# Layer two's probabilities turned by way of DRAM, its value products three panels behind, and three panels at once at the head of a stage

## The chip, the cores and the metric

The kernel runs on one core of a Trainium2 chip. The metric is device microseconds of one execution, the median of some runs. Engines are called as in the profile: PE is TensorE (PEld its weight loads), DVE VectorE, ACT ScalarE, POOL GpSimd; SP only issues DMAs. Every engine works through its own queue in order and waits at an instruction until what it needs is there.

## The reference, cut to what matters

Two decoder layers over 256 tokens of width 2048, all in float32. Layer 1 mixes with gated linear attention (GLA), layer 2 with forgetting attention (FoX, 12 heads of 128, keys and values computed once before the layer). Each layer also attends with four heads to 256 memory tokens, and each ends with a gated MLP of 5632 hidden units with a causal convolution of width 3.

```python
def memory_attention(q, mem_k, mem_v):            # 4 heads, 256 x 256 probabilities
    s = einsum('bhqd,bhkd->bhqk', heads(q), mem_k) * HD ** -0.5
    return merge(einsum('bhqk,bhkd->bhqd', softmax(s), mem_v))

def fox_attention(q, k, v, c):                    # 12 heads, causal
    s = einsum('bhqd,bhkd->bhqk', q, k) * HD ** -0.5
    s = s + c[t] - c[s]                           # sums of log forget gates
    return einsum('bhqk,bhkd->bhqd', softmax(where(causal, s, -inf)), v)

def fox_mixer(h, fk, fv, fc, mem_k, mem_v, w_in, w_out):
    q, mq = split_cols(h @ w_in, [1536, 512])
    return concat([fox_attention(q, fk, fv, fc),
                   memory_attention(mq, mem_k, mem_v)]) @ w_out

for i in range(2):                                # i = 0: gla_mixer, i = 1: fox_mixer
    x = x + mixer(rmsnorm(x), ...)
    u = causal_dwconv(rmsnorm(x) @ w_up[i])       # a, val = halves of u
    x = x + (silu(a) * val) @ w_down[i]
return rmsnorm(x)
```

## The kernel before, in words

**Weights and panels.** Every projection is cut into panels, a panel into units of 128 x 1024 float32 (512 KB). `split_unit` (lines 189 to 208) loads a unit into one of four `raw` buffers by a DMA from SP, rounds it on ACT to an fp32r part `whi` and subtracts that on DVE to give `wlo`; there are four buffers of each. So the kernel can hold four split units and four raw ones ahead of PE. Activations lie feature-major as two fp32r parts side by side (`bufA`, `bufB`: 16 tiles of 128 x 2 x 256, one for each block of 128 features). `proj_fm` computes 256 output features of all 256 tokens (4 units): per unit 8 matmuls of 512 columns with `whi` (line 242) and 8 of 256 columns with `wlo` (line 240). `proj_tm` (line 285) computes token-major panels of up to 512 features (8 units of 12 matmuls).

**Order.** The program is traced once; a planner gives each engine its fixed order by simulated time and by a priority that is the place in the program. `tc.high_priority(offset)` moves a piece forward by `offset` places (`AHEAD` is 300; unit loads and casts carry it), `tc.issue_after` ties an instruction behind another on its engine.

**The head of a stage.** The stages before the two MLPs and before FoX end with a token-major product added to `x` (`add_out`, four panels f = 0 to 3). After each, `preparing.then(f, b)` adds the squares for the norm, turns 32 x 32 blocks of `x` on DVE (line 1006, `blk`), moves the blocks between partitions with 16 DMAs (`move`, line 434, tile `turn`) and splits the result into the next stage's input (`split_turned`: ACT line 331, DVE line 333). For f = 3 all this has priority 2 x AHEAD, half of the moves are issued from ACT, and the norm's row (`n.row`, PE line 400, ACT line 403) is made with priority. The next stage starts with `pair_fm`: of two panels the units 0 to 2 come first, which need only feature blocks 0 to 11, and unit 3 of both (blocks 12 to 15, which come from f = 3) last. The second panel accumulates in the two PSUM banks of tag "s".

**Layer 2's attention.** `fox` takes eight query panels of two heads: two of memory queries, then six of FoX queries. When a panel ends, its evacuation makes q and scores (PE lines 455 for memory, 908 and 909 for FoX), the softmax on DVE and ACT, and turns the probabilities on PE against an identity matrix (`turn_blocks`, line 477: four 128 x 128 blocks for a memory head, three for a FoX head, PSUM bank "t"). A copy brings them to SBUF (ACT line 922; for memory the two parts of lines 441 and 442), the product with the values follows on PE (lines 455, or 925 and 926, bank "o"), and `split` writes the head's two parts into `mix`. The output projection (`("wo", 1, f)`) reads `mix` blocks 12 to 15 first, then 0 to 11.

**GLA.** For a head, `core` computes the scores inside the head, `outputs` the product with values and `scale` the norm; the order of the heads' pieces on PE is tied by `issue_after`.

Of the kernel before, what the change touches and what calls it, by code (L numbers as in the profile page):

```python
# [12 lines left out]
F32 = mybir.dt.float32  # L13
F32R = mybir.dt.float32r
# [5 lines left out]
P = 128  # L20
# [120 lines left out]
def _trunk(ctx: ExitStack, tc: tile.TileContext, xt, xtok, memt, wp, wgu, gns, gfin, cnv, par, msk, out):  # L141
# [71 lines left out]

    def pair_fm(keys, src, evacs):

        head = [(u, low) for u, low in ((0, 0), (1, 0), (0, 1), (1, 1), (2, 1), (2, 0))]
        panels_fm(keys, src, evacs, [(p, *t) for p in range(2) for t in head]
                  + [(0, 3, 0), (0, 3, 1), (1, 3, 1), (1, 3, 0)])

    def panels_fm(keys, src, evacs, turns, between=None):  # L220

        units = [where[key] for key in keys]

        acc = [[work("s", 2) if p else pacc.tile([P, 512], F32, name="acc", tag="acc") for _ in range(2)]
               for p in range(len(keys))]
        base = min(min(u[1]) for u in units[0])
        ready = {}
        for at, (p, u, low) in enumerate(turns):
            if (p, u) not in ready:
                ready[p, u] = split_unit(units[p][u])  # L230
                if u == 1 and between is not None:
                    between()
            end = all(t[0] != p for t in turns[at + 1 :])
            w = ready[p, u][low]
            for j, kc in enumerate(units[p][u][1]):
                both = src[kc - base]
                for c in range(2):
                    s = slice(j * 256 + c * P, j * 256 + (c + 1) * P)
                    if low:
                        TE.matmul(acc[p][c][:, :T], w[:, s], both[:, 0, :], start=False, stop=end and j == 3)  # L240
                    else:
                        TE.matmul(acc[p][c], w[:, s], both, start=u == j == 0, stop=end and j == 3)  # L242
# [13 lines left out]
    def proj_tm(key, src, evac, spare=None, first=None):  # L256
# [10 lines left out]
        for i in range(len(units) + ahead):  # L267
# [13 lines left out]
            for b, u, low, j in steps:  # L281
                kcs = units[u][1]
                w = ready[u][low][:, j * n : (j + 1) * n]
                for part in range(2 - low):
                    mm = TE.matmul(acc[b][:, :n], src[kcs[j] - base][:, part, b * P : (b + 1) * P], w,  # L285
                                   start=u == 0 and low == part == j == 0,
                                   stop=u == end and low == 1 and j == len(kcs) - 1)
                if u == end and low and j == len(kcs) - 1:
                    ends.append(mm)
                    evac(b, acc[b][:, :n])  # L290

    def turned(pool, bank, width, col, parts=False):
# [136 lines left out]

    def move(dst, src, on_act):  # L430

        for q in range(4):
            for c in range(4):
                (nc.scalar if on_act(q, c) else nc.sync).dma_start(  # L434
                    dst[32 * c : 32 * (c + 1), q], src[32 * q : 32 * (q + 1), c])

    def some(q, c):
# [35 lines left out]

    def turn_blocks(p, pt):

        for j, c in enumerate(pt):
            TE.transpose(c, p[:, j * P : (j + 1) * P], ident)  # L477

    def mem_product(kv, hd, pts):
# [5 lines left out]
        return po[:, :T]  # L485

    def mem_attention(pool, kv, q, hd, dst):

        q2 = [pool.tile([P, T], F32R, name="mqp", tag="tmp", bufs=5) for _ in range(2)]
        halves(q2, q)  # L490
        pt = work("t")
        for b in range(2):
            turn_blocks(mem_softmax(pool, kv, q2, hd, b), [pt[:, j * T + b * P : j * T + (b + 1) * P] for j in range(2)])
        pts = [pool.tile([P, 512], F32R, name="pts", tag="ed", bufs=2) for _ in range(2)]
        halves(pts, pt)
        split(dst, 12 + hd, mem_product(kv, hd, pts))

# [104 lines left out]
    def gla(nx):  # L602
        h, mix = bufB, bufA
        with tc.tile_pool(name="gla", bufs=1) as gp:
# [73 lines left out]
            def core(hd, q, k, bc, ahead):  # L678
# [125 lines left out]
            for hd in range(GLA_H):  # L804
# [18 lines left out]
                if hd:  # L823
                    proj_tm(("gv", hd), h, lambda b, a: S.activation(
                        v[:, b, :], a, AF.Copy, scale=nx.col()[:, b : b + 1]))
                core(hd, q, k, bc, ends[-1] if hd == 0 else made[1].spread if hd < GLA_H - 1 else made[3])
                vs = v
            for j in range(OG_EARLY, 6):
                if j == OG_EARLY + 2:
                    scale(*outputs(hd, vs))  # L830
                take_og(j)


    def fox(nx, vt, stash):
        hk, hq, mix = bufB, bufA, bufB
        with (
# [7 lines left out]

            pair_fm([("fk", j) for j in range(2)], hk, [fk_out(j) for j in range(2)])
            for j in range(6):
                if j > 1:
# [34 lines left out]

            def take_mq(j):
                def evac(c, a):
                    q = fp.tile([P, T], F32, name="mq", tag="tmp", bufs=5)
                    held.append(V.scalar_tensor_tensor(q, whole(a), -(HD ** -0.5), nx.row(), ALU.mult, ALU.mult))
                    mem_attention(fp, kv, q, 2 * j + c, mix)

                proj_fm(("mq", 1, j), hq, evac)

            held = []
            for j in range(2):
                take_mq(j)

            nc.sync.dma_start(cdram, cs[:FOX_H, :])

            def attend(hd, q):
# [11 lines left out]
                TE.matmul(ps[:, P : 3 * P], q[:, P:], kt[:, hd, :], start=True, stop=True)  # L909
                pt = work("t")  # L910
                for b in range(2):
# [10 lines left out]
                S.activation(pts, pt[:, : 3 * P], AF.Copy)  # L922
                po = work("o")
                hs = slice(hd * HD, (hd + 1) * HD)
                TE.matmul(po[:, :T], vt[:, 0, hs], pts[:, :T], start=True, stop=False)  # L925
                TE.matmul(po[:, P:T], vt[:, 1, hs], pts[:, T:], start=False, stop=True)
                if hd < 8:
                    mix[hd] = place("B", hd, "mix")
                split(mix, hd, po[:, :T])

            def take_q(j):
                def evac(c, a):
                    q = fp.tile([P, T], F32, name="fq", tag="fq", bufs=3)
                    V.scalar_tensor_tensor(q, whole(a), -(HD ** -0.5), nx.row(), ALU.mult, ALU.mult)
                    attend(2 * j + c, q)

                proj_fm(("fq", j), hq, evac)

            for j in range(6):
                take_q(j)  # L940


    def add_out(key, src, then=None, spare=None, last=None):
        for f in range(4):
            def evac(b, a, f=f):
                V.tensor_tensor(x[f][:, b, :], x[f][:, b, :], a, ALU.add)
                if then is not None:
                    then(f, b)

            proj_tm((*key, f), src, last if f == 3 and last is not None else evac, spare if f == 3 else None)  # L950

    def ffn(l, nx, h, m, then, spare=None, last=None):
        with tc.tile_pool(name=f"ffn{l}", bufs=1) as fp:
# [6 lines left out]
            for p, (lo, hi) in enumerate(PARTS):  # L960
# [22 lines left out]
                if p == 0:  # L983
                    first = 2
                    pair_fm([("up", l, j) for j in range(2)], h, [up_out(j, j) for j in range(2)])
                for j in range(lo + first, hi):
# [4 lines left out]
    def preparing(name, dst, pool, kept=None, second=None):  # L991
# [47 lines left out]
    with tc.tile_pool(name="turn2", bufs=1) as tp:  # L1039
        n, then = preparing("ffn1", bufA, tp)  # L1040
        add_out(("wo", 1), bufB, then)

# [117 lines left out]
```

## Time and profile before

| | |
|---|---|
| median of 3 runs | 2270.67 us (2270.03 to 2271.11) |
| profiled execution | 2270.71 us |
| its span, first to last instruction | 2268.9 us |
| granted TensorE clock | 0.999 |
| PE busy | 2255.7 us (99%) |
| DVE busy | 1610.5 us (71%) |
| ACT busy | 1255.9 us (55%) |
| data moved | 437.56 MB, mean 193 GB/s |

Stages on the span: memory projections and the first GLA panel to about 120 us, the rest of GLA to 374, its output projection to 461, MLP 1 to 1192, FoX keys and values to 1327, the eight query panels to 1438, the output projection to 1530, MLP 2 to 2261. A matmul's listed duration holds its pipeline, so that durations overlap; what one costs PE is read from the chain of waits, where consecutive pieces do not overlap.

### The profile page before, as it was taken

What the parts mean: (1) busy time and instruction counts of PE and PEld (TensorE: products, weight loads), DVE (VectorE), ACT (ScalarE), POOL (GpSimd) and SP (SyncE); (2) the same over time, 40 slices, a digit from 0 to 9 for tenths busy, and PEclk for the clock granted to TensorE, in tenths of its full rate; (3) what the DMA queues carried; (4) which work ended last, traced back from release to release, by engine and by line L of the source; (5) the groups of instructions that cost most, each with busy time, mean ns of one, the idle gap of its engine ahead of it and who ended that gap; (6) DMA issues with size and microseconds to landing.
All of it is one profiled execution on the core that took longest, in us unless ns stands there. A gap on an engine that the chain in (4) does not pass through costs nothing.

```text
span 2268.9 us, 33551 instructions
## 1 busy us (share of the span) xinstructions
PE 2255.7 (99%) x12305; PEld 1972.1 (87%) x12305; DVE 1610.5 (71%) x2714; ACT 1255.9 (55%) x1998; POOL 3.4 (0%) x19
## 2 busy tenths in 40 slices
PE   9999999999999999999999999999999999999998
PEld 8889998888888888888888998888888888888887
DVE  7779877677765777557777567668776577756775
ACT  6656675555543555445555555555554455534554
POOL 0000000000000000000000000000000000000000
PEclk9999999999999999999999999999999999999999
DMA  9555545655555555555566664476556555555554
GB/s 338 200 185 164 180 164 174 214 195 192 191 198 188 191 189 186 201 189 186 194 219 195 184 197 162 156 226 209 186 190 199 186 189 193 193 196 186 189 194 146
DMA packets 136365, 437.56 MB, mean 193 GB/s; under 512 B 17788, under 2 KB 30216, under 8 KB 136072
## 3 DMA queue, kind: packets, MB, share of 16 engines
q1 hardware_dynamic: 133896, 433.45, 57.5%
q10 hardware_dynamic: 2304, 1.98, 0.3%
q8 instruction: 96, 1.57, 0.3%
q14 instruction: 69, 0.57, 0.1%
HBM read 425.90 MB, written 2.11 MB: 189 GB/s over the span
## 4 chain that ended last, share of the span: by engine, by line
PE 92%; DMA 3%; DVE 2%; ACT 2%; SPq 1%; issue 1%; DVEq 0%; ACTq 0%
PE acc L242 36%; PE acc L285 34%; PE acc L240 19%; DMA raw<-wp 3%; DVE wlo L206 1%; ACT whi L205 1%; SPq L434 1%; PE ps_s L242 0%; DMA turn<-blk 0%; PE ps_s L240 0%; PE ps_s L734 0%; PE ps_o L455 0%; PE ps_s L455 0%; PE ps_t L477 0%; PE ps_o L925 0%
## 5 line engine op out<-in xcount | busy, mean ns | idle before, releaser
L206 DVE TENSOR_TENSOR wlo<-raw,whi 128x1024 fp32r<-128x1024 f32 (+4 forms) x809 | 968.6, 1200 | 544.9 <-ACT whi L205 448.7
L205 ACT ACTIVATE whi<-raw 128x1024 fp32r<-128x1024 f32 (+4 forms) x809 | 839.0, 1039 | 607.7 <-PE acc L285 325.0
L242 PE MATMUL acc<-B,whi 128*128 128x512 f32 x2048 | 484.0, 390 | 0.0
L242 PEld LDWEIGHTS acc<-B,whi 128*128 128x128 f32 x2048 | 378.9, 188 | 75.1
L285 PE MATMUL acc<-whi,mix 128*128 128x512 f32 x1280 | 319.7, 390 | 0.0
L242 PE MATMUL acc<-mix,whi 128*128 128x512 f32 x1224 | 297.8, 391 | 0.0
L285 PEld LDWEIGHTS acc<-whi,mix 128*128 128x128 f32 x1280 | 240.2, 188 | 49.7
L242 PEld LDWEIGHTS acc<-mix,whi 128*128 128x128 f32 x1224 | 226.0, 188 | 44.4
L240 PEld LDWEIGHTS acc<-B,wlo 128*128 128x128 f32 x2048 | 255.7, 191 | 5.4
L240 PE MATMUL acc<-B,wlo 128*128 128x256 f32 x2048 | 259.2, 283 | 0.0
L285 PE MATMUL acc<-whi,B 128*128 128x512 f32 (+3 forms) x960 | 217.0, 362 | 0.0
L285 PEld LDWEIGHTS acc<-whi,B 128*128 128x128 f32 x960 | 174.6, 188 | 18.3 <-ACT whi L205 0.3
L285 PE MATMUL acc<-wlo,mix 128*128 128x512 f32 x640 | 173.4, 389 | 0.0
L240 PE MATMUL acc<-mix,wlo 128*128 128x256 f32 x1224 | 159.9, 284 | 0.0
L240 PEld LDWEIGHTS acc<-mix,wlo 128*128 128x128 f32 x1224 | 155.5, 191 | 4.4
L285 PEld LDWEIGHTS acc<-wlo,mix 128*128 128x128 f32 x640 | 120.0, 188 | 24.9
L242 PE MATMUL acc<-A,whi 128*128 128x512 f32 x536 | 132.2, 390 | 0.0
L285 PE MATMUL acc<-wlo,B 128*128 128x512 f32 (+3 forms) x480 | 120.2, 362 | 0.0
L251 ACT ACTIVATE part<-acc 128x256 f32<-128x256 f32 x238 | 89.3, 378 | 55.3 <-PE acc L242 55.1
L242 PEld LDWEIGHTS acc<-A,whi 128*128 128x128 f32 x536 | 100.0, 188 | 20.4
L320 ACT ACTIVATE mix<-cv 128x256 fp32r<-128x256 f32 x60 | 25.0, 417 | 149.9 <-DVE cv L977 149.9
L971 ACT ACTIVATE cv<-u,cw 128x256 f32<-128x256 f32 x176 | 104.7, 596 | 4.9 <-DVE u L967 4.8
(246 smaller groups left out, 1736.1 us busy)
## 6 DMA issues: line engine op xcount, KB each, us to landing
raw<-wp SPq DMA_DIRECT2D x743, 512.0 KB, 3.6
raw<-wp SPq DMA_DIRECT2D x32, 384.0 KB, 3.3
raw<-wp SPq DMA_DIRECT2D x24, 388.0 KB, 3.6
turn<-blk SPq DMA_DIRECT2D x120, 32.0 KB, 3.5
raw<-wp SPq DMA_DIRECT2D x8, 400.0 KB, 3.1
xf<-xt SPq DMA_DIRECT2D x16, 128.0 KB, 5.3
x<-xtok SPq DMA_DIRECT2D x4, 512.0 KB, 9.3
mt<-memt SPq DMA_DIRECT2D x7, 256.0 KB, 6.3
```

What stands on the lines that cost most here:

```text
L205: casts.append(S.activation(hi[:, s], raw[:, s], AF.Copy))
L206: V.tensor_tensor(lo[:, s], raw[:, s], hi[:, s].bitcast(F32), ALU.subtract)
L240: TE.matmul(acc[p][c][:, :T], w[:, s], both[:, 0, :], start=False, stop=end and j == 3)
L242: TE.matmul(acc[p][c], w[:, s], both, start=u == j == 0, stop=end and j == 3)
L251: S.activation(t, a[:, T:], AF.Copy)
L285: mm = TE.matmul(acc[b][:, :n], src[kcs[j] - base][:, part, b * P : (b + 1) * P], w, start=u == 0 and low == part == j == 0, stop=u == end ...
L320: S.activation(hi, src, AF.Copy)
L434: (nc.scalar if on_act(q, c) else nc.sync).dma_start(dst[32 * c : 32 * (c + 1), q], src[32 * q : 32 * (q + 1), c])
L971: S.activation(r, u[:, 2:], AF.Identity, bias=w[3], scale=w[2])
```

## The change

- `pair_fm` becomes `three_fm`: units 0 to 2 of three panels, then unit 3 of all three. The third panel takes the other two accumulator banks. Only the first panel's evacuation keeps its priority. It is used at the three places where `pair_fm` was.
- In `preparing.then`, for f = 3 the priority goes from 2 x AHEAD to AHEAD, all 16 moves are issued from SP, and `n.row()` has no priority of its own.
- In layer 2 the PE transposes go. DVE turns 32 x 32 blocks of the probabilities (as layer 1's memory heads have it, line 504) into `ys`; for each panel of two heads, `move_far` writes the whole tile to DRAM with one DMA and reads it back with four that permute the blocks, into one of three `zs`. `values(pair)`, the products of a pair with its split into `mix`, is called when the panel three places later ends. FoX products read their moving operand from `zs` by blocks, and one of them writes PSUM by blocks.
- The last three pairs' products stand among the first two panels of the output projection, which are taken together: units 0 to 4 of f = 0, products of pair 5, units 0 to 4 of f = 1 with the products of pairs 6 and 7, then units 5 to 7 of both. `then` for f = 0 and 1 is called behind them.
- In GLA `core` of the last head is called one panel later, and the tie to the last matmul of the panel before is left out for the heads between.

```diff
-    def pair_fm(keys, src, evacs):
+    def three_fm(keys, src, evacs):
         head = [(u, low) for u, low in ((0, 0), (1, 0), (0, 1), (1, 1), (2, 1), (2, 0))]
-        panels_fm(keys, src, evacs, [(p, *t) for p in range(2) for t in head]
-                  + [(0, 3, 0), (0, 3, 1), (1, 3, 1), (1, 3, 0)])
+        panels_fm(keys, src, evacs, [(p, *t) for p in range(3) for t in head]
+                  + [(0, 3, 1), (0, 3, 0), (1, 3, 0), (1, 3, 1), (2, 3, 1), (2, 3, 0)])
...
-        acc = [[work("s", 2) if p else pacc.tile([P, 512], F32, name="acc", tag="acc") for _ in range(2)]
+        acc = [[work("s", 2) if p == 1 else pacc.tile([P, 512], F32, name="acc", tag="acc") for _ in range(2)]
...
             if end:
-                with tc.high_priority(offset=2 * AHEAD if len(keys) > 1 else 0):
+                ends.append(mm)
+                with tc.high_priority(offset=2 * AHEAD if len(keys) > 1 and p == 0 else 0):
...
+    def panel_tm(key, src, evac):
...
+        def step(i):
...
+            for b, low in passes:
+                for j, kc in enumerate(units[i][1]):
+                    for part in range(2 - low):
+                        mm = TE.matmul(acc[b][:, :n], src[kc - base][:, part, b * P : (b + 1) * P],
+                                       ready[low][:, j * n : (j + 1) * n], start=i == low == part == j == 0,
+                                       stop=i == end and low == 1 and j == len(units[i][1]) - 1)
...
+    def move_far(pool, dst, src, n):
+        far = pool.tile([P, 4 * T], F32, name="far", tag="far", bufs=2)
+        nc.sync.dma_start(far[:, : 4 * n], src[:, : 4 * n])
+        blocks = far[:, : 4 * n].rearrange("(q i) (c n) -> c i q n", q=4, c=4)
+        for c in range(4):
+            nc.sync.dma_start(dst[32 * c : 32 * (c + 1), : 4 * n].rearrange("i (q n) -> i q n", q=4), blocks[c])
...
-                    with tc.issue_after(ends[-1].ins), tc.issue_after(ahead.ins):
+                    with tc.issue_after(ahead.ins):
...
-                core(hd, q, k, bc, ends[-1] if hd == 0 else made[1].spread if hd < GLA_H - 1 else made[3])
+                if hd < GLA_H - 1:
+                    core(hd, q, k, bc, made[1].spread if hd else ends[-1])
...
                 take_og(j)
+                if j == OG_EARLY:
+                    core(hd, q, k, bc, ends[-1])
...
+            def values(pair):
+                z = zs[pair % 3]
+                if pair < 2:
+                    mem_values(fp, kv, pair, by_blocks(z), mix)
+                    return
+                z = narrow(z)
+                for hd in range(2 * pair - 4, 2 * pair - 2):
+                    zh = z[:, :, hd % 2]
+                    po = work("o")
+                    hs = slice(hd * HD, (hd + 1) * HD)
+                    TE.matmul(po[:, :T], vt[:, 0, hs], zh[:, :, :2, :].rearrange("p q n j -> p q (n j)"),
+                              start=True, stop=False)
+                    TE.matmul(po[:, :T].rearrange("p (q n j) -> p q n j", q=4, n=2)[:, :, 1, :], vt[:, 1, hs],
+                              zh[:, :, 2, :], start=False, stop=True)
...
+            def take(pair, head):
+                def evac(c, a):
+                    if c == 0 and pair >= BEHIND:
+                        values(pair - BEHIND)
+                    head(c, a)
+                    if c:
+                        move_far(dp, zs[pair % 3], ys[pair % 2], T if pair < 2 else 6 * 32)
...
-                    turn_blocks(lg, [pt[:, j * T + (b - j) * P : j * T + (b - j + 1) * P] for j in range(b + 1)])
-                pts = fp.tile([P, 3 * P], F32, name="fpt", tag="fpt", bufs=2)
-                S.activation(pts, pt[:, : 3 * P], AF.Copy)
...
+                    V.transpose(y[:, :, hd % 2, b : 2 * b + 1, :],
+                                lg[:, :n].rearrange("p (k c i) -> p c k i", c=4, i=32))
...
+            then_values = {(0, 4): 5, (1, 2): 6, (1, 4): 7}
+            steps = [panel_tm(("wo", 1, f), mix, add_to(f)) for f in range(2)]
+            for f in range(2):
+                for u in range(5):
+                    steps[f](u)
+                    if (f, u) in then_values:
+                        values(then_values[f, u])
+            for f in range(2):
+                for u in range(5, 8):
+                    steps[f](u)
...
-            with tc.high_priority(offset=2 * AHEAD if f == 3 else 0):
+            with tc.high_priority(offset=AHEAD if f == 3 else 0):
...
-                move(z, y, lambda q, c: f == 3 and c % 2)
+                move(z, y)
...
             if f == 3:
-                with tc.high_priority(offset=AHEAD):
-                    n.row()
+                n.row()
...
+        for f in range(2):
+            for b in range(2):
+                then(f, b)
+        add_out(("wo", 1), bufB, then, first=2)
```

More of the change, by code (lines that the diff above doesn't have):

```diff
@@ L290, in proj_tm, with add_to @@
                     evac(b, acc[b][:, :n])
+    def panel_tm(key, src, evac):
+        units = where[key]
+        n = units[0][2]
+        base = min(min(u[1]) for u in units)
+        acc = []
+        end = len(units) - 1
+        def step(i):
+            if i == 0:
+                acc.extend(pacc.tile([P, 512], F32, name="acc", tag="acc") for _ in range(2))
+            ready = split_unit(units[i])
+            passes = [(b, low) for low in range(2) for b in range(2)]
+            if i == end:
+                passes.sort()
+            for b, low in passes:
[4 more added lines that the diff above has]
+                                       stop=i == end and low == 1 and j == len(units[i][1]) - 1)
+                if i == end and low:
+                    ends.append(mm)
+                    evac(b, acc[b][:, :n])
+        return step
+    def add_to(f):
+        return lambda b, a: V.tensor_tensor(x[f][:, b, :], x[f][:, b, :], a, ALU.add)
     def turned(pool, bank, width, col, parts=False):
@@ L428, in place, with move @@
         return const.tile([P, 2, T], dtype, name=f"{name}{i}", tag=f"{buf}{i}")
-    def move(dst, src, on_act):
+    def move(dst, src, on_act=lambda q, c: False):
         for q in range(4):
@@ L485, in mem_product @@
         return po[:, :T]
[L487 to L496, printed above, removed]
     def mem_scores(pool, kv, q, hd, y):
@@ L886, in evac @@
                     held.append(V.scalar_tensor_tensor(q, whole(a), -(HD ** -0.5), nx.row(), ALU.mult, ALU.mult))
-                    mem_attention(fp, kv, q, 2 * j + c, mix)
-                proj_fm(("mq", 1, j), hq, evac)
+                    mem_scores(fp, kv, q, 2 * pair + c, by_blocks(ys[pair % 2]))
+                return head
             held = []
-            for j in range(2):
-                take_mq(j)
+            for pair in range(2):
+                take(pair, mem_head(pair))
             nc.sync.dma_start(cdram, cs[:FOX_H, :])
@@ L983, in ffn @@
                 if p == 0:
-                    first = 2
-                    pair_fm([("up", l, j) for j in range(2)], h, [up_out(j, j) for j in range(2)])
+                    first = 3
+                    three_fm([("up", l, j) for j in range(3)], h, [up_out(j, j) for j in range(3)])
                 for j in range(lo + first, hi):
```

52 lines of the change are left out of this document (26 added, 26 removed).

## The prediction

> **What bounds the kernel now.** The profiled execution took 2270.71 us, 0.04 over the median of 2270.67, so the sum is made against 2270.71 and holds for the median too; 1.8 us of it lie outside the span. I read the head of the page first, then the stretches, then who waited on PE.
>
> ```profile
> span 2268.9 us, 33551 instructions
> PE 2255.7 (99%) x12305; PEld 1972.1 (87%) x12305; DVE 1610.5 (71%) x2714; ACT 1255.9 (55%) x1998; POOL 3.4 (0%) x19
> ```
>
> ```profile
> 0.00:75.00 75.00, 72.91 (x373) 61.73 (x374) 56.62 (x98) 56.16 (x106) 0.75 (x7) 1.00 0.84 300
> ...
> 75.00:2260.00 2185.00, 2181.85 (x11931) 1909.97 (x11930) 1550.43 (x2605) 1197.94 (x1887) 2.66 (x12) 1.00 0.57 189
> 1326.96:1437.81 110.85, 110.85 (x674) 99.14 (x673) 82.09 (x208) 64.34 (x133) 0.00 (x0) 1.00 0.51 166
> 1349.00:1371.00 22.00, 22.00 (x140) 19.81 (x139) 19.67 (x44) 14.50 (x31) 0.00 (x0) 1.00 0.50 160
> ```
>
> ```profile
> PE ps_s L240 <- ACT B L331: 1.5, 1, 1.5
> PE ps_s L240 <- ACT A L331: 1.5, 1, 1.5
> ...
> PE ps_s L734 <- ACT later L782: 0.2, 1, 0.2
> ```
>
> The columns of the stretches are length, then PE, PEld, DVE and ACT busy. From 75 us to the end of the last matmul PE idles 3.15 us of 2185, and the waits name them: 1.47 us at the head of each MLP (rows below) and 0.2 in GLA. Outside of the ramp (the first 75 us, first row) PE is full everywhere at a granted clock of 1.00, also while the query panels run (third row). So there are two ways to win: take matmuls away, or those 3.15 us; and PE's order must not get a new wait.
>
> **The change, part by part.** *Transposes on PE.* What a PE instruction costs is read from the chain, not from its duration.
>
> ```profile
> L477 PE MATMUL ps_t<-mask,lg x36: 270/272/273, 1381.0 to 1458.2; 128*128 128x128 f32 x36
> L477 PE MATMUL ps_t<-mask,p x16: 271/272/274, 1351.4 to 1373.2; 128*128 128x128 f32 x16
> ```
>
> ```profile
> 1330.63 3.83 PE acc L240 x32
> 1334.46 7.28 PE acc L242 x32
> ...
> 1351.52 0.44 PE ps_t L477 x4
> ...
> 1381.20 0.33 PE ps_t L477 x3
> ...
> 1399.99 0.43 PE ps_o L925 x2
> 1400.42 0.22 PE ps_o L926 x2
> ...
> 1437.81 0.46 PE acc L285 x2
> ...
> 1464.12 59.87 PE acc L285 x264
> ```
>
> All 52 go: 52 x 0.11 = **5.7 us** off PE. Every other matmul stays. [...] The chain's 0.11 is what PE spends between its neighbours, and I go by it.
>
> *Turning on DVE and by DMA.*
>
> ```profile
> L206 DVE TENSOR_TENSOR wlo<-raw,whi 128x1024 fp32r<-128x1024 f32 (+4 forms) x809 | 968.6, 1200 | 544.9 <-ACT whi L205 448.7
> ```
>
> ```profile
> L504 DVE STREAM_TRANSPOSE y<-p x8: 431/442/448, 133.3 to 167.3; 128x256 f32<-128x256 f32 x8
> ```
>
> ```profile
> L472 DVE TENSOR_SCALAR lg<-lg,rc 128x128 f32<-128x128 f32 x10 | 2.7, 274 | 0.0
> ...
> L321 DVE TENSOR_TENSOR mix<-ps_o,mix 128x256 fp32r<-128x256 f32 x8 | 3.3, 413 | 0.4
> ```
>
> ```profile
> L922 ACT ACTIVATE fpt<-ps_t x12: 490/490/494, 1381.6 to 1458.5; 128x384 f32<-128x384 f32 x12
> ```
>
> Eight memory blocks of 128x256 at 0.44 and, for 12 FoX heads, 0.44 plus a 128x128 one, which before does not show: between nothing and 0.44, I take 0.28 as for the nearest 128x128 DVE operation: 3.5 + 8.6 = 12.2 us more on DVE. The 12 copies of 0.49 go from ACT (5.9 us off). The memory parts (two halves, one product) only move. In the stretch 1326.96 to 1437.81, DVE is busy 82.1 of 110.85. After, PE needs there 110.85 - 43 x 0.11 (36 + 16 less the 9 of the last three heads) - 6 x 0.65 (products, 0.43 + 0.22, that move behind the panels) = 102.2, and DVE 82.1 + 12.2 - 6 x 0.4 (their splits) = 91.9: 90%. The stretch of 22 us in the fourth row ran DVE at 89% and lost nothing on PE. So I cost this at nothing; without that cover it is rival 1. Products that read and write by blocks are not shown in before: the same columns, between no change and twice 0.65 x 12 = 7.8; I take none, since layer 1's products already are read out by blocks.
>
> *SP.* Each pair adds five DMAs (40 in all), and SP waits for the turned blocks before the first and for the landing before the other four.
>
> ```profile
> raw<-wp SPq DMA_DIRECT2D x743, 512.0 KB, 3.6
> ...
> turn<-blk SPq DMA_DIRECT2D x120, 32.0 KB, 3.5
> ```
>
> ```profile
> SPq L200 <- DVE wlo L206: 23.8, 10, 4.3
> ```
>
> Priced by these two, a hold is 3.6 + 5 x 0.59 (row below) = 6.6 us a pair, and the round trip 3.6 + 3.0 + 3.5 = 10.1. Behind SP stand unit loads. In 1371 to 1440 they already wait 23.8 us for a raw buffer that DVE must free (last row): they are as early as they can be, up to eight units ahead of PE, 8 x 12 x 59.87 / 264 = 21.8 us. So a hold of 6.6 costs nothing. [...]
>
> *Products later.* Three panels are over 33 us for a round trip of 10.1, nothing waits. Only the last pair is closer: in before its last probabilities are ready on DVE 11 us after the last panel (row below, against 1437.81 in the chain).
>
> ```profile
> 1448.45 0.35 DVE L472 TENSOR_SCALAR lg<-lg,rc 128x256 f32<-128x256 f32 x1
> ```
>
> With 2 us for the turns they are home at 11 + 2 + 10.1 = 23 us, and PE comes to them after ten units and four products, 10 x 2.72 + 4 x 0.65 = 29.8: 7 us in hand. Then two units, 5.4 us, cover their split before unit 7 reads it. Nothing; the interleaved panels do the same matmuls.
>
> *Head of the MLPs.*
>
> ```profile
> 480.00 1.19 PE L240 MATMUL ps_s<-B,wlo 128*128 128x256 f32 x8 [1.47 <-ACT B L331]
> ```
>
> ```profile
> 1544.29 0.28 PE L400 MATMUL ps_t<-dg,onesr 128*128 128x256 f32 x1
> ...
> 1548.71 1.19 PE L240 MATMUL ps_s<-A,wlo 128*128 128x256 f32 x8 [1.47 <-ACT A L331]
> ```
>
> ```profile
> 1535.65 6.28 ACTq L434 DMA_DIRECT2D turn<-blk  x8
> 1544.84 0.39 ACT L403 ACTIVATE row<-ps_t 128x256 f32<-128x256 f32 x1 [9.34 <-PE ps_t L400]
> 1545.12 2.00 ACT L205 ACTIVATE whi<-raw 128x1024 fp32r<-128x1024 f32 x2
> 1547.01 1.69 ACT L331 ACTIVATE A<-turn,gains 128x256 fp32r<-128x256 f32 x4
> ```
>
> ```profile
> 1535.02 0.33 SPq L200 DMA_DIRECT2D raw<-wp  x1
> ...
> 1535.64 5.96 SPq L434 DMA_DIRECT2D turn<-blk  x8
> 1542.11 6.81 SPq L200 DMA_DIRECT2D raw<-wp  x4
> ```
>
> ```profile
> L434 SPq DMA_DIRECT2D turn<-blk x120: 507/588/1525, 398.0 to 1541.0; - x120
> ```
>
> ACT stands at the row it was told to make early, which waits for two matmuls far back in PE's queue; casts and split come after it, and PE runs dry at 1547.24 for 1.47 us. The third panel gives PE three quarters of 11.11 = 8.3 us of work that needs no late block, so unit 3 is due at 1555.6; the row loses its priority. What is late next: 16 moves from SP alone take 16 x 0.59 = 9.4 us, until 1545.1, land at 1548.6 and are split by ACT (1.69) by 1550.3: 5 us in hand. Loads stand behind them; before the moves SP has issued the second unit of the third panel (1535.02), so the third one is loaded at 1545.1, lands at 1548.7, is split (1.0 on ACT, 1.2 on DVE) by 1551, and is due at 1547.24 + 2 x 1.82 + 2 x 0.96 = 1552.8: 2 us in hand. Both waits go: **2.9 us**. The FoX stage lost nothing at its head. The 8 ACT issues at each head stood in that same wait; that they go is no further gain.
>
> *GLA.* PE's order changes, not its work. The gain is at most the 0.2 us wait; a loss is bounded by the 1.5 us that such late splits cost elsewhere. I take 0.
>
> Sum: 2270.71 - 5.7 - 2.9 = **2262.1**.
>
> **The rivals.** *1, slower: DVE becomes the bound of the query panels.* PE's next score matmuls wait for a "s" bank that DVE frees; if the turns (0.72 a head) and a weight cast (1.2) stand ahead in DVE's queue each time, 12 x 1.9 = 23 us come on: about 2285. It makes the kernel slower from 13.2 us, 1.1 a head. For it: 90% on DVE in a fixed order, with the wait for ACT's exponentials in between. Against: the 89% row. [...]
> *2: the heads of the MLPs keep a wait*, since the loads behind 16 moves come later than I have them: 2265.0 with the old waits, 2268.6 with two of 3.3 us (third panel's third unit issued 5 us later).
> *3: the last products come late*, SP being held behind blocked loads: a round trip of 20 instead of 10 us gives 3 us on PE for each of the last two pairs, 2268.
> *4: the change doesn't do what it says:* PE is given less work but DVE's casts and the DMAs pace it just the same, 2270.7. Against: the waits name no cast outside the ramp.
>
> **How the numbers follow.** Forecast 0.50, rival 1 0.16, rival 2 0.14, rival 3 0.10, rival 4 0.10. A measurement tells some 0.2%, 4.5 us, from no change: below 2266.1 is faster, above 2275.2 slower. Faster: 0.50, most of 2 (0.10) and a little of 3: 0.62. Same: the rest of 2 and 3 and most of 4: 0.20. Slower: rival 1 and a little of 4: 0.18. The forecast's own range is 2259 (less 0.2 in GLA, 2.1 of PE's idle in the ramp if the new order moves it, 0.6 as the runs spread) to 2265; the whole one, to 2273, takes in rivals 2, 3 and 4 and leaves out rival 1.
>
> **What would show it.** Right: no line 477 on PE and its busy time about 6 us lower; no wait over 1 us at both heads of the MLPs, the row's wait on ACT short; DVE near 90% in the query panels and PE without waits there; the last pair's blocks in SBUF before PE asks. Wrong: waits of score matmuls on DVE, of products on the read-back DMAs, of `acc` on casts or loads behind SP's holds, or a PE busy time that falls by far more or less than 5.7.

## The result, and the profile after

The changed kernel takes 2263.27 us (median; 2262.81 to 2264.49) against 2270.47 (2270.03 to 2271.11) for the kernel before: 7.2 us less, a ratio of 0.9969 [0.9960, 0.9978]. The profiled execution took 2263.27 us, of which 1.9 lie outside the span. The forecast was 2262.1.

The head of the page of the changed kernel: span, then busy time, share and count of each engine.

```profile
span 2261.4 us, 33526 instructions
PE 2249.8 (99%) x12253; PEld 1967.1 (87%) x12253; DVE 1617.1 (72%) x2746; ACT 1250.7 (55%) x1986; POOL 3.4 (0%) x19
```

PE is busy 5.9 us less with exactly 52 matmuls fewer (12305 to 12253), DVE 6.6 more, ACT 5.2 less. Next, the waits of PE in the changed kernel (who waited for what: us in total, times, longest).

```profile
PE ps_o L180 <- DVE B L177: 1.4, 1, 1.4
PE acc L240 <- ACT mix L363: 1.2, 1, 1.2
PE acc L286 <- ACT whi L205: 0.7, 1, 0.7
PE ps_s L758 <- ACT later L806: 0.3, 1, 0.3
```

The first and third row lie in the ramp. In this execution both old waits of 1.47 us at the heads of the MLPs are gone, but a new one of 1.2 us stands in the second row, at the head of the second MLP. The stretches of the changed kernel (length, then PE, PEld, DVE, ACT and POOL busy, granted clock, DMA share, GB/s): from the ramp to the last matmul, the query panels, and the last 60 us of these.

```profile
75.00:2260.00 2185.00, 2176.98 (x11881) 1905.11 (x11879) 1560.23 (x2649) 1194.53 (x1880) 2.66 (x12) 1.00 0.59 193
1325.19:1429.25 104.06, 104.06 (x617) 92.73 (x617) 85.80 (x231) 58.12 (x121) 0.00 (x0) 1.00 0.69 222
1369.00:1429.00 60.00, 60.00 (x352) 53.46 (x352) 55.57 (x171) 33.64 (x78) 0.00 (x0) 1.00 0.74 235
```

(The first stretch has an emptier end only because the kernel ends earlier.) In the query panels PE is never idle, although DVE reaches 55.57 of 60 us, 93%. For the kernel before, the timeline of PE has the first matmuls of the second MLP here:

```profile
1530.17 3.79 PE L242 MATMUL acc<-mix,whi 128*128 128x512 f32 x16
```

In the changed kernel they start at 1522.89. So query panels and output projection together went from 1530.17 - 1326.96 = 203.2 us to 1522.89 - 1325.19 = 197.7: **5.5 us**, where 52 x 0.11 = 5.7 were forecast. The panels began 1.8 us earlier (1326.96 to 1325.19): the wait of 1.47 at the first MLP's head, and 0.3 from elsewhere. At the second MLP's head 1.47 went and 1.19 came. 5.5 + 1.8 + 0.3 makes 7.6, and the span is 7.5 us shorter.

### The profile page after: what moved, and what is told of

It reads as the page before. It is cut to its first block, busy times and chain, and to the rows that moved or that the text cites. A ratio compares the mean times of both kernels' runs of the same rounds, so it can differ in the third digit from the quotient of the medians.

```text
span 2261.4 us, 33526 instructions
## 1 busy us (share of the span) xinstructions
PE 2249.8 (99%) x12253; PEld 1967.1 (87%) x12253; DVE 1617.1 (72%) x2746; ACT 1250.7 (55%) x1986; POOL 3.4 (0%) x19
## 3 DMA queue, kind: packets, MB, share of 16 engines
q10 hardware_dynamic: 1152, 1.19, 0.2%
## 4 chain that ended last, share of the span: by engine, by line
PE 96%; ACT 1%; DVE 1%; DMA 1%; issue 0%; SPq 0%; DVEq 0%; ACTq 0%
PE acc L242 37%; PE acc L286 34%; PE acc L240 20%; PE acc L311 2%; PE ps_s L242 1%; PE ps_s L240 1%; DMA raw<-wp 0%; ACT whi L205 0%; DVE wlo L206 0%; PE ps_s L758 0%; PE ps_o L495 0%; PE ps_s L495 0%; PE ps_o L931 0%; PE ps_s L976 0%; ACT L822 0%
## 5 line engine op out<-in xcount | busy, mean ns | idle before, releaser
L286 PE MATMUL acc<-whi,mix 128*128 128x512 f32 x1216 | 302.5, 389 | 0.0
L286 PEld LDWEIGHTS acc<-whi,mix 128*128 128x128 f32 x1216 | 228.3, 188 | 47.4
L286 PE MATMUL acc<-whi,B 128*128 128x512 f32 (+3 forms) x896 | 200.5, 360 | 0.0
L286 PEld LDWEIGHTS acc<-whi,B 128*128 128x128 f32 x896 | 162.7, 188 | 15.9 <-ACT whi L205 0.3
L286 PE MATMUL acc<-wlo,mix 128*128 128x512 f32 x608 | 164.5, 389 | 0.0
L286 PEld LDWEIGHTS acc<-wlo,mix 128*128 128x128 f32 x608 | 114.1, 188 | 23.7
L286 PE MATMUL acc<-wlo,B 128*128 128x512 f32 (+3 forms) x448 | 111.6, 360 | 0.0
```

## The experiments

Each was timed against the kernel before on the same chip (2270.5 to 2270.7 in every set). "Before plus" and "after with" say which kernel was edited.

### What one transpose costs: before, with each transpose on PE done twice

```diff
-            TE.transpose(c, p[:, j * P : (j + 1) * P], ident)
+            for _ in range(2):
+                TE.transpose(c, p[:, j * P : (j + 1) * P], ident)
```

> The kernel before with each of the 52 transposes on PE issued twice into the same place. Theory: a transpose costs PE the 0.11 us of the chain: 2270.5 + 5.7 = 2276.2 (2275.5 to 2277.5). Rival: it costs its listed 0.272 us: 2270.5 + 14.1 = 2284.6.

Measured: 2276.4 us (2275.43 to 2277.21), a ratio of 1.0026 [1.0016, 1.0035], 5.8 us more. The page's line of engines and, from the timeline of line 478, the turns of FoX:

```profile
PE 2261.4 (99%) x12357; PEld 1978.0 (87%) x12357; DVE 1610.4 (71%) x2714; ACT 1255.8 (55%) x1998; POOL 3.4 (0%) x19
L478 PE MATMUL ps_t<-mask,lg x72: 270/272/273, 1382.4 to 1463.6; 128*128 128x128 f32 x72
```

52 more transposes are listed with 272 ns each, and PE's busy time rises by 5.7 us: 0.11 each, as the chain said. Priced at the listed duration they would have added 52 x 0.272 = 14.1 us, and the run refutes that.

### Is DVE near its limit: after, with each of DVE's new turns done twice

```diff
-            V.transpose(y[:, :, hd % 2, :, b, :], p.rearrange(...))
+            for _ in range(2 if pool.name == "fox" else 1):
+                V.transpose(y[:, :, hd % 2, :, b, :], p.rearrange(...))
...
-                    V.transpose(y[:, :, hd % 2, b : 2 * b + 1, :], lg[:, :n].rearrange(...))
+                    for _ in range(2):
+                        V.transpose(y[:, :, hd % 2, b : 2 * b + 1, :], lg[:, :n].rearrange(...))
```

> The changed kernel with every turn of layer 2's probabilities on DVE issued twice, some 12 us more on DVE in the query panels (DVE 85.8 of 104.1 us there before this, 55.6 of the 60 us from 1369 on). Theory: weights are so far ahead that even a DVE near or a little over 100% in that stretch costs PE little: 2263.3 to 2265. Rival 1 of the prediction (score matmuls wait for banks that DVE frees, 1.1 us a head or more): 2275 or more.

Measured: 2264.95 us (2262.56 to 2268.2), 0.9975 [0.9966, 0.9985]; its profiled execution took 2264.31. The two stretches of the query panels, and a wait of PE, in this kernel:

```profile
1325.19:1429.25 104.06, 103.59 (x615) 92.35 (x614) 88.78 (x237) 55.91 (x116) 0.00 (x0) 1.00 0.71 220
1369.00:1429.00 60.00, 59.53 (x353) 52.84 (x352) 55.24 (x170) 31.54 (x76) 0.00 (x0) 1.00 0.78 239
```

```profile
PE ps_s L976 <- ACT p L505: 0.5, 1, 0.5
```

PE loses 0.5 us in the panels. The 32 added turns raise DVE's busy time by 8.1 us in all (1617.1 to 1625.2), but only by 3.0 in the panels (85.80 to 88.78), and in the last 60 us it is the same 55 us: as much other work of DVE was done elsewhere. Rival 1, with 23 us, is refuted with its own cause doubled.

### The two halves alone

Before plus the new heads (three panels, the priorities and SP's moves of `then`), transposes left on PE; and after with the old heads (`pair_fm`, the old priorities, half of f = 3's moves issued from ACT):

```diff
# heads alone: before plus
-    def pair_fm(keys, src, evacs):
+    def three_fm(keys, src, evacs):
...
-            with tc.high_priority(offset=2 * AHEAD if f == 3 else 0):
+            with tc.high_priority(offset=AHEAD if f == 3 else 0):
-                move(z, y, lambda q, c: f == 3 and c % 2)
+                move(z, y, lambda q, c: False)
-                with tc.high_priority(offset=AHEAD):
-                    n.row()
+                n.row()
# turns alone: after, with these lines the other way round
```

> The kernel before with the heads of the stages alone: three panels at once, all moves of f = 3 from SP, the lower priorities. Theory: the two waits of 1.47 us go and nothing else changes, since the calls for f = 0 and 1 stay early: about 2267.5 us (2267.0 to 2268.2), no PE wait over 0.5 us at either MLP's head. Rival: the head's gain needs the rest of the change, or the wait only moves: 2269.5 to 2270.7.

> The changed kernel with the heads of before: two panels at once, half of f = 3's moves from ACT, the high priorities. Theory: 52 transposes x 0.11 = 5.7 us less on PE, the first MLP's head keeps its 1.47 us, the second keeps that or has a longer one, since f = 2's moves are late here too: 2264.7 to 2266.5. Rival (the gain sits in the heads, the turns give theirs back): 2268 or more.

Measured: heads alone 2268.56 us (2267.23 to 2269.4), 0.9992 [0.9982, 1.0001]; turns alone 2270.97 (2269.03 to 2273.19), 1.0001 [0.9992, 1.0011]. Both are slower than expected: heads alone by 0.4 us beyond its range and with a wait at the first head that was not to be there, turns alone by 4.5 us, in the rival's range. The parts are worth -2.0 (its interval just reaches no change) and +0.4, together -7.2: **they do not add**. The waits of PE, of heads alone and then of turns alone:

```profile
PE acc L240 <- DVE wlo L206: 1.0, 1, 1.0
```

```profile
PE ps_s L242 <- ACT whi L205: 6.0, 1, 6.0
PE ps_s L240 <- ACT B L363: 1.5, 1, 1.5
```

With the heads alone a wait of 1.0 for a weight cast stands at the first MLP and none at the second, so about 2.0 of the 2.9 come. With the turns alone the old 1.5 stays at the first MLP, and at the second one PE waits 6.0 us. ACT and PE in the timeline of turns alone at that place, then its stretches of 5 us:

```profile
1529.98 7.34 ACTq L466 DMA_DIRECT2D turn<-blk  x8
1537.36 0.38 ACT L435 ACTIVATE row<-ps_t 128x256 f32<-128x256 f32 x1 [9.82 <-DMA turn<-blk]
1537.64 2.94 ACT L205 ACTIVATE whi<-raw 128x1024 fp32r<-128x1024 f32 x3
1538.74 3.78 PE L242 MATMUL ps_s<-mix,whi 128*128 128x512 f32 x8 [5.96 <-ACT whi L205]
```

```profile
1535.00:1540.00 5.00, 1.25 (x3) 1.06 (x4) 1.28 (x2) 2.64 (x4) 0.00 (x0) 0.81 0.47 109
1540.00:1545.00 5.00, 5.00 (x19) 4.42 (x19) 5.00 (x16) 4.72 (x10) 0.00 (x0) 0.51 0.82 274
1545.00:1550.00 5.00, 5.00 (x33) 4.54 (x32) 3.33 (x5) 1.06 (x1) 0.00 (x0) 1.00 0.57 208
```

ACT stands at its own eight DMA issues and then makes the row; three casts, whose raw data were there, are behind them in its queue (second and third row). ACT did nothing else for 9.8 us, and PE ran dry for 6. After that the granted clock is 0.51 for five us: x19 matmuls instead of x33 in the same time, and PE's busy time is 2253.0 us, 3.2 more than in the changed kernel. The gap before it is 5.96 us long. A later run (blocks by way of DRAM, below) has a clock of 0.66 behind a gap of 2.14 us, and the kernel before 1.00 behind its two gaps of 1.47 us; between 1.47 and 2.14 no run shows it. Against the changed kernel's span of 2261.4 the sum is (6.0 - 1.2) + 1.5 + 3.2 = 9.5 us, and the span of turns alone is 2271.1. But this profiled execution took 2273.19 us, the slowest of its ten, 2.2 over their median: how long the others waited there is not in the trace.

### Who issues the moves: turns alone, with all of f = 3's moves from SP

```diff
-                move(z, y, lambda q, c: f == 3 and c % 2)
+                move(z, y)
```

> The turns alone (two panels, high priorities, as in the run before) but with all of f = 3's moves from SP. Theory: there the 6.0 us wait came because ACT, with casts queued behind, stood at its own DMA issues; freed of them the second head loses 1 to 3 us instead, and TensorE's clock does not drop: 2265.5 to 2268. Rival: ACT stands just as long at the early row, and the 6 us wait with its dip of the clock stays: 2270 or more.

Measured: 2265.29 us (2263.45 to 2268.44), 0.9978 [0.9969, 0.9987]. This one line is worth 5.7 us between 2270.97 and 2265.29. The waits of PE in it:

```profile
PE ps_s L240 <- ACT B L363: 1.3, 1, 1.3
PE acc L240 <- ACT mix L363: 0.9, 1, 0.9
```

The wait of 6.0 for a cast has gone and, with it, the clock's fall (1.00 in every 5 us there). What is left is the old wait at the first MLP and 0.9 us for a moved block at the second. The pair of panels and the row's priority are still those of the old heads, so it was ACT's own issues that kept the turns' gain away.

### What the third panel is worth: after, with two panels

```diff
-            three_fm([("fk", j) for j in range(3)], hk, [fk_out(j) for j in range(3)])
+            pair_fm([("fk", j) for j in range(2)], hk, [fk_out(j) for j in range(2)])
...
-                    three_fm([("up", l, j) for j in range(3)], h, [up_out(j, j) for j in range(3)])
+                    pair_fm([("up", l, j) for j in range(2)], h, [up_out(j, j) for j in range(2)])
```

> The changed kernel with two panels at the heads instead of three, all else kept (all moves from SP, low priorities). Theory after the run with the turns alone: what ended the old waits is mostly that ACT is free of the early row and of its DMA issues; in the changed kernel ACT splits f = 3's first block at 478.6 and 1539.0, two panels would need it at 478.3 and 1540.8: waits of 0.5 to 1.5 us at the first head, 0 to 1 more at the second, 2263.5 to 2265.5. Rival, as in the prediction: the third panel's 8.3 us are what ends both waits; without it each is 1.5 us or more, 2266 and over.

Measured: 2265.55 us (2263.95 to 2267.89), 0.9979 [0.9969, 0.9988]. Its waits outside the ramp and GLA:

```profile
PE acc L240 <- ACT mix L363: 1.2, 1, 1.2
PE acc L240 <- ACT B L363: 0.6, 1, 0.6
```

The profiled execution was the lowest of its runs and lost only 0.6 us at the first head. The medians give the third panel 2.3 us (2265.55 to 2263.27), the trace 0.6; the executions of this kernel spread over 4 us, and what the others wait for isn't in the trace. The second head's 1.2 is the same with two panels as with three, so panels do not cover it.

### The new wait at the second head

In the changed kernel the chain of waits has, ahead of the wait, SP's last moves (start, length, what):

```profile
1525.69 0.59 SPq L466
...
1526.32 3.84 DMA turn<-blk
...
1530.38 0.52 ACT mix L363
...
1530.94 0.50 PE acc L240 x2
```

The block split at 1530.38 is of f = 2, not of f = 3. In the timeline of the changed kernel, why f = 2's moves are that late (DVE's turn, then SP):

```profile
1508.90 1.31 DVE L1077 STREAM_TRANSPOSE blk<-x 128x512 f32<-128x512 f32 x2 [3.35 <-DMA turn<-blk]
...
1513.48 1.14 SPq L466 DMA_DIRECT2D turn<-blk  x2
...
1525.14 11.99 SPq L466 DMA_DIRECT2D turn<-blk  x19
```

Of `blk` and `turn` there are two buffers each. `then` for f = 0 and f = 1 is now called behind both panels, so that f = 2's turn on DVE stands 3.35 us, until 1508.9, for moves of the earlier blocks to land, and its own moves start at 1513.5, nine us before PE is at the stage. In the kernel before, the stage began 7.3 us later, at 1530.17, and f = 2's blocks were split from here on:

```profile
1529.34 1.71 ACT L331 ACTIVATE mix<-turn,gains 128x256 fp32r<-128x256 f32 x4 [1.54 <-DMA turn<-blk]
```

The split is now only 1.0 us later. What changed more is that PE comes 7.3 us sooner, while the moves, which go out among SP's loads, do not. No run separates the late calls of `then` from PE's earlier arrival. Three of the 19 moves that begin at 1525.14 are still f = 2's. Two edits take work from SP there: half of f = 2's moves issued from ACT (timed twice, the second time beside the changed kernel), and f = 0 to 2 moved by way of DRAM with five DMAs each instead of 16.

```diff
# half of f = 2's moves from ACT: after with
-                move(z, y)
+                move(z, y, lambda q, c: f == 2 and name == "ffn1" and c % 2)
# by way of DRAM: after with, in the second MLP's head
-                move(z, y)
+                if far is not None and f < 3:
+                    move_far(far, z, y, T)        # both as 128 x 1024
+                else:
+                    move(z, y)
```

> The changed kernel with half of the 16 moves of f = 2 ahead of the second MLP issued from ACT. Theory: the 1.2 us wait at that head stands on SP's queue of moves (the last one of f = 2 issued 3.4 us after PE began the stage), 8 moves less are 4.7 us earlier, and the wait goes: 2262.1, no PE wait at the head. Rival: ACT, held by its own DMA issues as in the run with the turns alone, is late with the casts, and the wait stays or grows: 2263.3 to 2268.

> The changed kernel with the blocks of f = 0 to 2 ahead of the second MLP moved by way of DRAM (five DMAs each, as the probabilities) instead of with 16 small DMAs: 33 DMAs less on SP, some 19 us of its issue time. Theory: SP reaches f = 2 at once, its round trip is 6.1 + 4 x 0.43 + 2.9 = 11 us from the turned blocks (ready 12.7 us before PE begins the stage and 19 before it needs them), and the 1.2 us wait goes: 2262.1. Rival: the hold of SP for the landing delays the weights and the wait only changes its name: 2263.3 or more.

> The changed kernel itself, beside the others of this set: 2263.3 us, as before.

> The changed kernel with half of f = 2's moves ahead of the second MLP from ACT once more, now with the changed kernel on the same chip and in more rounds. Theory: without the 1.2 us wait it is 0.5 to 1.2 us faster than the changed kernel, 2262.1 to 2262.8. Rival: small waits elsewhere, 0.5 us each and others than in the changed kernel, take it back: 2263.3.

Measured: from ACT 2262.6 us (2261.55 to 2263.82), 0.9964 [0.9952, 0.9977], and again 2263.39 (2262.72 to 2263.7), 0.9967 [0.9954, 0.9979]; beside the second, the changed kernel once more 2263.19 (2262.75 to 2265.37), 0.9969 [0.9957, 0.9981]. By way of DRAM 2266.99 (2264.18 to 2270.08), 0.9985 [0.9975, 0.9994]. The waits of PE outside the ramp for longer than 0.2 us: from ACT the second time, the changed kernel again, and by way of DRAM.

```profile
PE acc L240 <- DVE wlo L206: 1.5, 1, 1.5
```

```profile
PE acc L240 <- ACT mix L363: 0.9, 1, 0.9
```

```profile
PE acc L242 <- ACT whi L205: 2.8, 2, 2.1
PE acc L240 <- DVE wlo L206: 1.0, 1, 1.0
```

With the moves on ACT the wait for `mix` is gone in both profiled executions. That fits its cause, but shows it only in part. The split of f = 2 begins 0.8 and 0.2 us earlier than in the changed kernel (1529.55 and 1530.18 against 1530.38), where 4.7 were expected, and PE reaches the stage 1.3 and 1.7 us later (1524.17 and 1524.62 against 1522.89). Counted from f = 2's first move the split comes after 15.1 and 14.7 us instead of 16.9, so the moves did get faster. But with DVE's turns doubled, where all moves stayed on SP, PE came at 1525.20 and did not wait for `mix` either: the wait hangs on when PE comes as much as on SP. And the time is not measurably lower beside the changed kernel (2263.39 to 2263.19), and in the profiled execution a wait of 1.5 stands at the *first* head, up to which the order of instructions is the same in both kernels. The chain of waits of that execution (half of f = 2's moves from ACT, the second time) says what it is:

```profile
479.68 3.53 DMA raw<-wp
...
484.40 1.24 DVE wlo L206
...
485.68 1.22 PE acc L240 x8
```

This is the load of a unit that stands behind SP's 16 moves. SP's moves there, in the changed kernel's profiled execution and then in this one:

```profile
466.02 10.76 SPq L466 DMA_DIRECT2D turn<-blk  x16
```

```profile
468.51 10.76 SPq L466 DMA_DIRECT2D turn<-blk  x16
```

They take the same 10.8 us, but begin 2.5 us later, and PE is at the stage at the same time to 0.2 us. One step back stands f = 2 again: DVE turns f = 3's `x`, which SP then moves, behind its part of the split of f = 2's blocks, and ACT begins that split here, in the changed kernel and then in this one:

```profile
459.71 1.71 ACT L363 ACTIVATE B<-turn,gains 128x256 fp32r<-128x256 f32 x4 [0.69 <-DMA turn<-blk]
```

```profile
462.20 1.71 ACT L363 ACTIVATE B<-turn,gains 128x256 fp32r<-128x256 f32 x4 [3.00 <-DMA raw<-wp]
```

That is the same 2.5 us. The last three moves of f = 2 were issued 0.9 us later (456.17 and 457.06); the rest is open. So the unit is either just in time or up to 1.5 us late, and late is the rule. Nine profiled executions have three panels and all of f = 3's moves from SP at this head: the changed kernel's two waited 0 and 0.2 us, the other seven 0.5 to 1.5 (0.5 and 1.5 with half of f = 2's moves on ACT, 1.0 heads alone, 1.0 by way of DRAM, 1.1 with DVE's turns doubled, and 1.2 and 0.9 in the two runs of the next section). The 1.2 us at the second head are real, but executions differ by as much at the first.

By way of DRAM SP has fewer issues at the second head, and PE waits 2.8 us there for casts (first row; the 1.0 is the first head's again). ACT and PE in its timeline, and a stretch of 5 us:

```profile
1521.00 1.71 ACT L363 ACTIVATE mix<-turn,gains 128x256 fp32r<-128x256 f32 x4 [7.09 <-DMA turn<-far]
...
1545.06 3.62 PE L242 MATMUL acc<-mix,whi 128*128 128x512 f32 x8 [2.14 <-ACT whi L205]
```

```profile
1545.00:1550.00 5.00, 4.94 (x21) 4.23 (x22) 3.96 (x4) 3.18 (x4) 0.00 (x0) 0.66 1.00 389
```

ACT stands 7.1 us at f = 2's blocks, which come back late, and DVE 6.4 us behind it; casts are queued behind both. By that f = 3's turn and its 16 moves come late as well, and the load behind these moves is what PE waits 2.1 us for. Behind that gap the granted clock is 0.66 for five us, and PE's busy time is 2251.8 us, 2.0 more than in the changed kernel. SP's stand at the landing of the writes, the rival's reason, is 5.2 us from 1480 to 1550, where it stands 33.7 us for raw buffers. No variant is distinctly faster than the changed kernel.

### The two free choices: one panel behind, and GLA's old order

```diff
# one panel behind: after with
-            PAIRS, BEHIND = 8, 3
+            PAIRS, BEHIND = 8, 1
-            then_values = {(0, 4): 5, (1, 2): 6, (1, 4): 7}
+            then_values = {(1, 4): 7}
# GLA's old order: after with
-                    with tc.issue_after(ahead.ins):
+                    with tc.issue_after(ends[-1].ins), tc.issue_after(ahead.ins):
-                if hd < GLA_H - 1:
-                    core(hd, q, k, bc, made[1].spread if hd else ends[-1])
+                core(hd, q, k, bc, ends[-1] if hd == 0 else made[1].spread if hd < GLA_H - 1 else made[3])
```

> The changed kernel with the products one panel behind instead of three (the last pair's stay where they are). In the changed kernel a pair's blocks are back in SBUF some 24 us after its panel ended, and panels are 13 us apart. Theory (the distance is needed): PE's queue has products about 10 us before their blocks, seven pairs, up to 70 us; as much of it as the planner does not put behind other matmuls is lost, 2270 to 2335. Rival: the planner sees the round trip and puts the products behind other matmuls, so the distance is not needed: 2263 to 2266.

> The changed kernel with layer 1's order as before (core of the last head called one panel earlier, the tie to the panel's last matmul back). Theory: worth nothing, 2263.3 give or take 0.6, the wait of line 758 on ACT stays at 0.2 to 0.6 us. Rival: part of the gain sits there: 2264.5 or more.

Measured: one behind 2263.51 us (2262.4 to 2264.4), 0.9969 [0.9956, 0.9981]; GLA's old order 2263.31 (2262.35 to 2263.49), 0.9966 [0.9954, 0.9979]. Neither differs from the changed kernel (2263.19 beside them). The products of FoX in the timelines, one panel behind and then three behind:

```profile
L931 PE MATMUL ps_o<-z,fvt x24: 377/379/383, 1398.6 to 1470.4; 128*128 128x256 f32 x24
```

```profile
L931 PE MATMUL ps_o<-z,fvt x24: 377/379/383, 1402.9 to 1474.4; 128*128 128x256 f32 x24
```

The products come only 4 us earlier when they are called two panels earlier, and none of them is among PE's waits: the planner sets them behind other matmuls until their blocks are home. Only the memory pairs' products wait, twice for 0.5 us together (line 495, for ACT's copy of blocks that came late). So the distance of three panels hides at most that; it is not what hides the round trip.

## Why the prediction was right, and where it was not

The time is 1.2 us above the forecast and inside the forecast's own range. By its steps:

**Transposes on PE, 5.7 us.** Right. 5.5 us in the stretch, 5.9 in PE's busy time, and 5.8 for as many added.

**Turning on DVE at no cost.** Right. The 128x128 turn, estimated at 0.28 us, is listed with 0.30 on the mean. DVE is busy 82% of the panels (85.80 of 104.06), not 90%, but 93% of the last 60 us. Its busy time rose by 6.6 us in all, where 12.2 were priced from listed durations: these overlap on DVE as they do on PE (two turns of 128x256, listed with 0.43 each, fill 0.64 us together; the same 32 turns once more added 8.1). PE was the full engine (busy 99% of the span before), and in the query panels it is busy 104.06 of 104.06 us with the turns on DVE.

**SP's hold, 6.6 us a pair, at no cost.** The conclusion was right, the terms weren't. From the list of DMAs of the changed kernel (KB each, median us from issue to landing), then SP's waits in 1325 to 1480:

```profile
far<-y SPq DMA_DIRECT2D x6, 384.0 KB, 6.1
z<-far SPq DMA_DIRECT2D x24, 96.0 KB, 2.9
```

```profile
SPq L200 <- DVE wlo L206: 43.8, 17, 6.4
SPq L475 <- DMA far<-y: 29.1, 8, 5.9
```

The write lands after 6.1 us, not the 3.6 of a unit load, and an issue of a read takes 0.43, not 0.59. SP stands 3.6 us a pair at that landing (second row, eight pairs). In the same time it stands 43.8 us waiting for a raw buffer, so it had the hold to spare.

**Products later, 7 us in hand.** Right, with the size off. SP's last four reads and PE's last two products in the timeline of the changed kernel:

```profile
1449.63 1.75 SPq L475 DMA_DIRECT2D z<-far  x4
...
1469.85 0.60 PE L931 MATMUL ps_o<-z,fvt 128*128 128x256 f32 x2
...
1474.16 0.60 PE L931 MATMUL ps_o<-z,fvt 128*128 128x256 f32 x2
```

The reads are issued by 1451.4 and with 2.9 home by 1454.3, 15.5 us before the first of the two. And the distance of three, on which the step leaned, did not matter: called one panel behind, FoX's products wait no more than before, and the memory pairs' 0.5 us.

**Heads of the MLPs, 2.9 us.** Here the prediction failed, by the 1.2 us of the new wait. Both old waits went, as it said. In the list of "what is late next" it weighed f = 3's moves and the loads behind them, with 5 and 2 us in hand, and left out f = 2's moves, though the change calls `then` for f = 0 and 1 behind both panels; that move got no price. It put f = 2's blocks behind the buffers of f = 0 and 1, and PE, which the removed transposes bring there 7 us sooner, overtook them. The 2 us in hand for the loads, worked out at the second head alone, were too many at the first: there the load behind the moves was 0.5 to 1.5 us late in seven of nine executions, and in time (0 and 0.2) in the changed kernel's two. So the 1.47 us there are not won as surely as these two suggest. The waits of both heads together are 1.2 and 1.1 us in them, and 0.5 to 1.7 in five of the seven (all but heads alone and by way of DRAM).

**"That they go is no further gain",** said of ACT's issues, was wrong. The sentence took the wait before (1.47) as all that they could cost. In the new order the same issues, with the casts behind them, cost 6.0 us and the clock's fall behind it in the profiled execution, and 5.7 us by the medians; giving them to SP is what lets the 5.7 us of the transposes be kept. The sum came out because the change does both, which is luck in this step: for the turns alone the same working gives 2270.7 - 5.7 = 2265.0, 6 us too low.

**GLA, 0.** Right (2263.31 with the old order).

**The rivals.** 1 is refuted by the doubled turns; 3 by the last pair's rows; 4 by the time. Rival 2, a wait at the heads for loads behind the 16 moves, happened at the first head in seven of nine executions, at 0.5 to 1.5 us; the larger wait, at the second head, had another cause.

## What to carry to other kernels

Price a matmul that is taken away by the distance between its neighbours in the chain, not by its listed duration (0.11 against 0.27 us here). When a full engine is made faster, ask of every supplier of the next stage whether that engine paces it: SP's moves were bound to their own buffers and issues, did not come earlier with PE, and became the next wait (1.2 us at the second head). Where an engine issues DMAs in order with casts behind them, look whether those DMAs are ready when their turn comes (with the turns alone PE waits 6.0 us for such a cast, with the same moves from SP for none); a part that measures as worth nothing alone may be what the other part needs.

## What was not expected of the hardware

- A gap of 6 us on PE cost about 9 in one execution: the granted clock was 0.51 in the 5 us behind it, and PE was busy 3.2 us longer (2253.0 against 2249.8) for the same matmuls. By way of DRAM a gap of 2.14 us was enough for a clock of 0.66 in the 5 us behind it. The two gaps of 1.47 us in the kernel before left the clock at 1.00.
- In the changed kernel the writes of 384 KB from SBUF to DRAM landed after 6.1 us (median of six), while unit loads of 512 KB took 3.8.
- Two executions with the same order of instructions differ by 1.5 us at one head, because SP begins its 16 moves 2.5 us later in one (466.0 and 468.5), as ACT does the split ahead of them (459.7 and 462.2). Why those blocks landed later is open, as is the spread of 4 us of the kernel with two panels.
